# Other addresses for the low halves of the weights, and another order of products in layer two, in a two-layer hybrid encoder trunk

## The chip, the cores and the metric

The kernel runs on one core of one Trainium2 chip, as one launch. The metric is the device time of a launch in microseconds. Three timed runs stand for the kernel before, and one further execution was recorded by the profiler; all durations of single instructions come from that one.

## What is computed

The reference is a trunk of two layers on 256 tokens plus 16 learned meta tokens, with a model width of 2048. Cut to what matters:

```python
def _layer(h, ...):
    proj = einsum('bld,dp->blp', h, w_in)            # 2048 x 6176: GLA q, k, v, gate, decay and NA q, k, v
    y_gla = _gla_mixer(...)                          # bidirectional gated linear attention, 4 heads
    y_na = _na_mixer(...)                            # 2-D neighbourhood attention, 16 heads
    mix = einsum('blm,md->bld', concat([y_gla, y_na]), w_out)
    h = layer_norm(ALPHA * h + mix)
    ff = square(relu(h @ w_ff1)) @ w_ff2             # 2048 -> 8192 -> 2048
    return layer_norm(ALPHA * h + ff)
```

Everything is float32. By far the most arithmetic lies in the four weight matrices `w_in`, `w_out`, `w_ff1` and `w_ff2`; attention and norms are small beside them.

## The kernel before

**Split products.** A float32 product is made of products in a reduced format (float32r). Each weight tile and each activation tile is split into a high half (a rounding cast) and a low half (the rest). The sum is `wh*xh + wh*xl + wl*xh`. Activations lie transposed, 128 features on the partitions and tokens along the free axis, so a weight block of 128x128 is the stationary operand and 256 to 274 columns of tokens are the moving one.

**Weight tiles.** The stream of weights (`order`, line 153) is cut into tiles of 128 partitions x 1024 floats, that is eight blocks of 128x128. `made` (line 180) issues the DMA of a tile into `raw` on the SP queue, and `halves` (line 208) casts it to `wh` on ACT (line 211, L211 in the profile) and subtracts `raw - wh` into `wl` on DVE (line 212, L212). Each of `raw`, `wh` and `wl` has three buffers, and `weights` (line 174) keeps two tiles ahead of the one in use.

**Where a block lies.** `blocks` (line 194) gives the place of block j within the tile's row in SBUF: `first + j//2 * pair + j%2 * step` floats. For `wh` that is `0, 128, 256, ...`, blocks one behind the other. For `wl` the three numbers come from `LOWS` (line 42), by whether the tile is one of layer two's "once" tiles. Since `pair` is 320 floats (1280 bytes), the blocks of a tile stand at two places past a multiple of 256 bytes, by turns. Before the change these are 64 and 192 bytes for "once" tiles, and 0 and 192 bytes for all others. The start of each `wl` tile is a multiple of 256 bytes, and so are the starts of `wh` blocks.

**Two forms of the products of a tile.** `by_m` (line 276 on) makes one output tile after another, each from all its weight tiles. For each weight tile it calls `eight` (line 232), which runs through the string in `TURNS` (line 43) and issues one product for each letter (L246 in the profile): `h` is `wh` with the high half of the activations, `l` is `wh` with their low half, `w` is `wl` with their high half.

- In layer one, with 272 tokens (a few groups with 274), and in those products of layer two that still need the meta tokens (272 or 258 columns) or that are named as slim, the string is `hlhlwwhlhlww...`: 24 products, four on `wh` and two on `wl` by turns.
- In layer two most outputs need 256 tokens only. There a tile is "once": high and low half of the activations are laid side by side, and one `h` product of 512 columns makes `wh*xh` and `wh*xl` together; `w` is a product of 256 columns. A tile has eight `h` and eight `w`. Before the change the string is `hhhhhhhhwwwwwwww`: all eight 512-column products, then all eight of 256 columns.

In layer two's attention the halves of the activations that feed these 512-column products stand 288 floats apart (`pair`, line 303, without `dense`), in its output projection and its MLP they are contiguous.

`by_k` (line 257 on, L272) is another form, in which one pair of blocks serves four outputs. It reads the same kind of tiles and isn't touched, but for the place of the odd `wl` blocks.

**What sets the order around it.** Instructions are recorded engine by engine. Between the weight tiles `pump` (line 124) gives steps of attention and norms to the engines; where layer-two attention stands in this, a scheduler may put neighbouring small instructions of ACT, DVE, POOL and SP in another order when PE's order changes.

Of the kernel before, what the change touches and what calls it, by code (L numbers as in the profile page):

```python
# [14 lines left out]
P = 128  # L15
# [23 lines left out]
PAD = 40  # L39
PITCH = 288  # L40
WIDE = 1280
LOWS = {True: (16, P + 32, 2 * P + 64), False: (0, P + 48, 2 * P + 64)}
TURNS = {True: "hhhhhhhhwwwwwwww", False: "hlhlwwhlhlwwhlhlwwhlhlww"}


class Pair(tuple):
# [10 lines left out]
class Trunk:  # L57
# [122 lines left out]
    def made(self, ap, ends, once):  # L180
# [4 lines left out]
        wh, wl = self.wp.tile([P, WB], F32R, name="wh", tag="wh"), self.wp.tile([P, WIDE], F32R, name="wl", tag="wl")  # L185
        wh, wl = self.blocks(wh, 0, P, 2 * P), self.blocks(wl, *LOWS[once])
        for c in map(slice, (0,) + ends, ends):
# [44 lines left out]
    def eight(self, ps, wh, wl, x, n, first, last, once):  # L232
# [5 lines left out]
        seen = dict.fromkeys("hlw", 0)  # L238
        for i, kind in enumerate(TURNS[once]):
            j = seen[kind]  # L240
# [3 lines left out]
            if once:  # L244
                rhs, o = (v.once, ps) if kind == "h" else (v[0][:, :T], ps[:, T:])
            mm(o, lhsT=self.block(w, j), rhs=rhs, start=first and not i, stop=last and i == len(TURNS[once]) - 1)  # L246

# [958 lines left out]
```

## Time and profile before

| what | value |
|---|---|
| median of three runs | 2359.66 us (2359.44 to 2359.98) |
| the profiled execution's own time | 2360.16 us |
| its span in the trace | 2358.4 us |
| granted TensorE clock, mean | 0.999 |
| PE busy, weight loads busy | 2348.3 us, 2234.0 us |
| DVE busy, ACT busy | 1523.6 us, 1213.4 us |
| matrix products issued | 18180 |

The span is the time from the first to the last instruction; 1.8 us of the execution's own time lie around it. A product is busy from its start to its modelled end, and since products are pipelined the busy times of neighbours overlap. The rate at which PE really goes is therefore read from starts: in the timeline view each row has the start of a group of equal neighbouring instructions (us), the busy time, and how many there are, and the difference of two starts divided by the number of products between them is the time per product.

### The profile page before, as it was taken

To read this page: it belongs to the slowest core of one execution; us is meant where nothing else is said; L and a number is where in the kernel's file an instruction comes from. 1 tells how busy PE (TensorE), PEld (TensorE's weight loads), DVE (VectorE), ACT (ScalarE), POOL (GpSimd) and SP (SyncE) were. 2 spreads that over 40 slices of the span, in tenths; PEclk is the share of its full clock that TensorE was granted. 3 is DMA by queue.
4 is the path that set the end of the run, shared out by engine and by line. 5 is a ranking of instruction groups with operands and counts; after the bars stand their busy time and mean duration, and the time that the engine had idled before them with its cause. 6 is when DMAs were issued, how large, how long until landed. Compare 5 with 4: busy or idle time off the path is not lost.

```text
span 2358.4 us, 44599 instructions
## 1 busy us (share of the span) xinstructions
PE 2348.3 (100%) x18180; PEld 2234.0 (95%) x18180; DVE 1523.6 (65%) x2432; ACT 1213.4 (51%) x2100; POOL 131.4 (6%) x200
## 2 busy tenths in 40 slices
PE   9999999999999999999999999999999999999998
PEld 9999999999999999999999999999988888888888
DVE  5588777775544455546567787778866545666655
ACT  5666664564433344444457666655654333444443
POOL 0021110110000000000020111100100000000000
PEclk9999999999999999999999999999999999999999
DMA  8454445555555555555555555456566666666664
GB/s 260 153 160 153 151 141 171 170 178 179 176 174 177 177 174 178 178 175 176 177 184 160 174 167 154 156 159 199 182 194 191 193 189 194 189 192 211 202 192 146
DMA packets 118301, 419.02 MB, mean 178 GB/s; under 512 B 13512, under 2 KB 14024, under 8 KB 118096
## 3 DMA queue, kind: packets, MB, share of 16 engines
q1 hardware_dynamic: 117808, 415.65, 56.4%
q8 instruction: 142, 2.33, 0.4%
q10 hardware_dynamic: 288, 0.52, 0.1%
q14 instruction: 63, 0.52, 0.1%
HBM read 414.03 MB, written 2.10 MB: 176 GB/s over the span
## 4 chain that ended last, share of the span: by engine, by line
PE 97%; DVE 2%; issue 1%; ACT 1%; POOL 0%; DVEq 0%; ACTq 0%; POOLq 0%
PE mm L246 85%; PE mm L272 6%; PE bg L272 1%; PE bg L783 1%; PE mm L722 1%; PE bg L583 0%; DVE wl L212 0%; PE bg L429 0%; PE mm L748 0%; DVE acc L1011 0%; ACT wh L211 0%; PE mm L472 0%; PE bg L909 0%; PE bg L634 0%; PE bg L664 0%
## 5 line engine op out<-in xcount | busy, mean ns | idle before, releaser
L212 DVE TENSOR_TENSOR wl<-raw,wh 128x1024 fp32r<-128x1024 f32 (+1 forms) x770 | 942.6, 1225 | 649.1 <-ACT wh L211 644.6
L211 ACT CAST wh<-raw 128x1024 fp32r<-128x1024 f32 (+1 forms) x770 | 805.1, 1047 | 926.8 <-PE mm L246 579.5
L246 PE MATMUL mm<-x,wh 128*128 128x272 f32 (+3 forms) x5376 | 990.5, 311 | 0.0
L246 PEld LDWEIGHTS mm<-x,wh 128*128 128x128 f32 x5376 | 798.4, 188 | 38.6 <-PE mm L722 0.6
L246 PE MATMUL mm<-x,wl 128*128 128x272 f32 (+3 forms) x3264 | 590.1, 284 | 0.0
L246 PEld LDWEIGHTS mm<-x,wl 128*128 128x128 f32 x3264 | 485.4, 188 | 11.4
L246 PE MATMUL mm<-y,wh 128*128 128x272 f32 (+2 forms) x2128 | 411.4, 322 | 0.0
L246 PEld LDWEIGHTS mm<-y,wh 128*128 128x128 f32 x2128 | 325.4, 188 | 22.0
L246 PE MATMUL mm<-u,wh 128*128 128x272 f32 (+2 forms) x1552 | 299.1, 321 | 0.0
L246 PEld LDWEIGHTS mm<-u,wh 128*128 128x128 f32 x1552 | 237.1, 188 | 16.0
L246 PE MATMUL mm<-y,wl 128*128 128x272 f32 (+1 forms) x1408 | 240.5, 282 | 0.0
L246 PEld LDWEIGHTS mm<-y,wl 128*128 128x128 f32 x1408 | 204.3, 188 | 6.4
L246 PE MATMUL mm<-u,wl 128*128 128x272 f32 (+1 forms) x1024 | 175.2, 282 | 0.0
L246 PEld LDWEIGHTS mm<-u,wl 128*128 128x128 f32 x1024 | 148.8, 188 | 4.7
L272 PE MATMUL mm<-x,wh 128*128 128x272 f32 (+1 forms) x512 | 73.5, 289 | 0.0
L272 PEld LDWEIGHTS mm<-x,wh 128*128 128x128 f32 x512 | 67.9, 191 | 0.0
L999 POOL TENSOR_SCALAR acc<-acc,vec 128x272 f32<-128x272 f32 (+1 forms) x24 | 41.9, 1751 | 273.9 <-DVE acc L1011 154.2
L871 DVE TENSOR_TENSOR acc<-acc,mm 128x256 f32<-128x256 f32 (+1 forms) x71 | 30.1, 424 | 38.9 <-PE mm L246 38.9
L560 ACT COPY U<-S 128x272 f32<-128x272 f32 (+1 forms) x104 | 41.0, 429 | 19.3 <-DVE S L569 18.3
L569 DVE TENSOR_TENSOR S<-S,dec 128x272 f32<-128x272 f32 (+1 forms) x112 | 46.1, 441 | 3.7 <-ACT U L560 3.1
L294 ACT CAST u<-ft 128x272 fp32r<-128x272 f32 (+1 forms) x64 | 26.1, 408 | 41.7 <-DVE ft L827 41.7
L571 POOL TENSOR_TENSOR dec<-dec 128x272 f32<-128x272 f32 (+6 forms) x56 | 29.9, 534 | 245.9 <-DVE S L569 245.9
(265 smaller groups left out, 1634.4 us busy)
## 6 DMA issues: line engine op xcount, KB each, us to landing
raw<-in_wff SPq DMA_DIRECT2D x512, 512.0 KB, 3.6
raw<-in_win SPq DMA_DIRECT2D x190, 512.0 KB, 3.9
raw<-in_wout SPq DMA_DIRECT2D x64, 512.0 KB, 3.6
nb<-in_nab SPq DMA_DIRECT2D x16, 352.0 KB, 4.1
xraw<-in_xT SPq DMA_DIRECT2D x7, 272.0 KB, 5.5
out<-out SPq DMA_DIRECT2D x5, 256.0 KB, 3.2
brow<-in_norm SPq DMA_DIRECT2D x4, 256.0 KB, 4.9
gw<-in_wup SPq DMA_DIRECT2D x4, 196.0 KB
```

What stands on the lines that cost most here:

```text
L211: self.nc.scalar.copy(h, r)
L212: self.wl = self.nc.vector.tensor_tensor(lo, r, h.bitcast(F32), ALU.subtract).ins
L246: mm(o, lhsT=self.block(w, j), rhs=rhs, start=first and not i, stop=last and i == len(TURNS[once]) - 1)
L272: self.nc.tensor.matmul(ps[g + m][:, :n], lhsT=self.block(parts[p][0], 4 * j + m), rhs=acts[k + j][parts[p][1]][:, :n], start=k + j + p == ...
L294: self.nc.scalar.copy(hi, src)
L560: nc.scalar.copy(U[:, lv % 4, j, :w].rearrange("p (n t h) -> p n t h", t=2, h=hb), bass.AP(S.tensor, S.offset + 2 * j * L, [S.ap[0], [2 * ...
L569: tt(o, o, totals(lv, odd, w), ALU.mult)
L571: nc.gpsimd.tensor_tensor(d[1], d[1], d[0], ALU.mult)
L722: nc.tensor.matmul(ps[hh][:, t * NKEY:t * NKEY + NKEY], lhsT=q[hs, NM + t * P:NM + t * P + P], rhs=k[hs, t, :], start=True, stop=True)
L783: nc.tensor.matmul(po[t][hs, :P], lhsT=v2[ts, hs] if rest else v1[:, t, hs], rhs=p2[ts, hh, :] if rest else p1[:, 2 * hh + t, :], start=re ...
L871: tt(a, a, part, ALU.add)
L999: nc.gpsimd.tensor_scalar(a, a, gain, bias, ALU.mult, ALU.add)
```

## The change

Three numbers and one string differ. The low blocks of "once" tiles move from 64 and 192 bytes past a multiple of 256 to 32 and 160. The odd low blocks of all other tiles move from 192 to 64; the even ones stay at 0. And in "once" tiles the eight `h` and eight `w` products alternate: the two products of block 0, then those of block 1, and so on. The number of instructions of these kinds, their shapes and their operands stay the same, and so do the sums, apart from the order in which they are added.

```diff
-LOWS = {True: (16, P + 32, 2 * P + 64), False: (0, P + 48, 2 * P + 64)}
-TURNS = {True: "hhhhhhhhwwwwwwww", False: "hlhlwwhlhlwwhlhlwwhlhlww"}
+LOWS = {True: (8, P + 32, 2 * P + 64), False: (0, P + 16, 2 * P + 64)}
+TURNS = {True: "hwhwhwhwhwhwhwhw", False: "hlhlwwhlhlwwhlhlwwhlhlww"}
```

The code that reads the two tables is unchanged:

```python
wh, wl = self.blocks(wh, 0, P, 2 * P), self.blocks(wl, *LOWS[once])
...
for i, kind in enumerate(TURNS[once]):
```

## The prediction

> **What bounds the kernel now.** I read the page first: the busy times, the granted clock, and the chain that ended last.
>
> ```profile
> span 2358.4 us, 44599 instructions
> ...
> PE 2348.3 (100%) x18180; PEld 2234.0 (95%) x18180; DVE 1523.6 (65%) x2432; ACT 1213.4 (51%) x2100; POOL 131.4 (6%) x200
> ...
> PEclk9999999999999999999999999999999999999999
> ...
> PE 97%; DVE 2%; issue 1%; ACT 1%; POOL 0%; DVEq 0%; ACTq 0%; POOLq 0%
> ```
>
> PE is never without work, its clock is full in every slice, and 97% of the chain is PE. No other engine's work or wait is worth anything unless it stops PE. So the only question is how fast PE goes through products whose number and shape don't change. For that I read starts in the timeline, first in layer two's MLP (512- and 256-column products, ACT and DVE rows of the weight split between them).
>
> ```profile
> 1801.18 1.08 PE L246 MATMUL mm<-x,wl 128*128 128x256 f32 x8
> ...
> 1802.09 2.00 PE L246 MATMUL mm<-x,wh 128*128 128x512 f32 x8
> ...
> 1803.93 1.08 PE L246 MATMUL mm<-x,wl 128*128 128x256 f32 x8
> 1804.18 1.05 ACT L211 CAST wh<-raw 128x1024 fp32r<-128x1024 f32 x1 [1.40 <-issue]
> 1804.85 2.00 PE L246 MATMUL mm<-x,wh 128*128 128x512 f32 x8
> ...
> 1805.26 1.22 DVE L212 TENSOR_TENSOR wl<-raw,wh 128x1024 fp32r<-128x1024 f32 x1 [1.19 <-ACT wh L211]
> ...
> 1810.35 2.00 PE L246 MATMUL mm<-x,wh 128*128 128x512 f32 x8
> ```
>
> A tile's eight `h` take 1803.93 - 1802.09 = 1.84 us, 230 ns each; its eight `w` take 0.91 to 0.92 us, 114.3 ns each. From 1802.09 to 1810.35 are three tiles: **2.753 us a tile**. The same sixteen products in layer two's attention:
>
> ```profile
> 1458.19 2.02 PE L246 MATMUL mm<-x,wh 128*128 128x512 f32 x8
> 1460.04 1.11 PE L246 MATMUL mm<-x,wl 128*128 128x256 f32 x8
> 1460.99 2.02 PE L246 MATMUL mm<-x,wh 128*128 128x512 f32 x8
> 1462.84 1.11 PE L246 MATMUL mm<-x,wl 128*128 128x256 f32 x8
> ```
>
> Here a tile takes 1460.99 - 1458.19 = **2.80 us**: `w` 0.95 us (118.8 ns each), `h` 1.85 us. Same instructions, same weight addresses; what differs is that the halves of the activations lie apart. Next, the 272-column products: two stretches with the same string, one in layer two's attention (timeline), and layer one's long ones (the windows view: from:to, length, PE busy and count).
>
> ```profile
> 1448.45 0.41 PE L246 MATMUL mm<-x,wl 128*128 128x272 f32 x2
> 1448.69 0.65 PE L246 MATMUL mm<-x,wh 128*128 128x272 f32 x4
> ...
> 1454.31 0.41 PE L246 MATMUL mm<-x,wl 128*128 128x272 f32 x2
> ```
>
> ```profile
> 393.00:531.00 138.00, 138.00 (x1104) 138.00 (x1102) 106.42 (x183) 78.43 (x129) 14.59 (x8) 1.00 0.56 176
> 531.00:1071.00 540.00, 540.00 (x4329) 540.00 (x4328) 271.56 (x306) 222.44 (x299) 0.00 (x0) 1.00 0.56 177
> 1071.00:1222.00 151.00, 151.00 (x1209) 150.82 (x1209) 92.10 (x143) 66.31 (x88) 2.21 (x9) 1.00 0.59 184
> ```
>
> From 1448.45 to 1454.31 are eight sixes, 48 products: 122.1 ns each. In layer one 829 us hold 6642 products: 124.8 ns each. PE doesn't wait in either, the shapes are equal, and yet one rhythm is 2.2% slower. The lesson of these views is that a product costs its columns and then some nanoseconds that depend on how products and weight loads follow each other. This is the part of the time that the change can touch, and its size is the whole argument.
>
> **The change part by part.** How many tiles are there? Products of 512 columns (groups of the whole trace; the last row is the attention's part, 1222 to 1580 us):
>
> ```profile
> L246 PE MATMUL mm<-x,wh 128*128 128x512 f32 x1152 | 289.8, 394 | 0.0
> L246 PE MATMUL mm<-y,wh 128*128 128x512 f32 x688 | 172.5, 392 | 0.0
> L246 PE MATMUL mm<-u,wh 128*128 128x512 f32 x496 | 124.1, 392 | 0.0
> ...
> L246 PE MATMUL mm<-x,wh 128*128 128x512 f32 x320 | 81.6, 397 | 0.0
> ```
>
> 2336 / 8 = 292 tiles: 40 at 2.80 us and 252 at 2.753 us.
>
> *The turns.* Now every `w` follows an `h` and every `h` a `w`. The trace shows how an `h` run settles (cuts of the timeline begun within the run that starts at 1804.85):
>
> ```profile
> 1805.32 0.62 PE L246 MATMUL mm<-x,wh 128*128 128x512 f32 x2
> ```
>
> ```profile
> 1806.01 0.84 PE L246 MATMUL mm<-x,wh 128*128 128x512 f32 x3
> 1806.69 0.28 PE L246 MATMUL mm<-x,wl 128*128 128x256 f32 x1
> ```
>
> The third `h` starts at 1805.32, the sixth at 1806.01, the first `w` at 1806.69: the first two `h` take 0.47 us (235 ns each), the first five 1.16 us (232 ns), the last three 0.68 us (227 ns). An `h` just after a `w` is dearer than one in a settled run. For `w` in mixed order there is the slim group at the end, the string of threes with 256 columns in all products:
>
> ```profile
> 2334.36 0.40 PE L246 MATMUL mm<-y,wl 128*128 128x256 f32 x2
> 2334.59 0.64 PE L246 MATMUL mm<-y,wh 128*128 128x256 f32 x4
> ...
> 2345.00 0.40 PE L246 MATMUL mm<-u,wl 128*128 128x256 f32 x2
> ```
>
> 15 sixes in 10.64 us: 118.2 ns a product of 256 columns, against 114.3 ns in a run of eight `w`. So I price the alternating tile at 8 x (231 + 118.2) = 2.794 us: `w` by the mixed row, `h` between the run's mean of 230 and the 232 of its first five. That is +0.041 us on 252 tiles and -0.006 us on 40: **+10.1 us**.
>
> *The low blocks at 32 and 160.* No row shows a block at such a place, so I give it no term of its own, and bound the two edits together. Below: all `h` as the last three of a run, all `w` as in a run of the MLP, 8 x (227 + 114.3) = 2.730 us; that is -0.023 x 252 - 0.070 x 40 = -8.6 us. Above: all `h` as the first two (235), all `w` as in the attention (118.8): 2.830 us, +0.077 x 252 + 0.030 x 40 = +20.6 us. I take the price above since its rows are those in which products of two kinds alternate.
>
> *The odd low blocks from 192 to 64* in all other tiles touch one of six products in a 272-column tile. Bounds: all 6642 products of layer one in the quicker rhythm, 6642 x 2.7 ns = -18 us; above, I know no slower rhythm of a long stretch and set +9 us, half of that, as an estimate. The row nearest to it is layer one as it is, with low blocks at 0 and 192 and the quicker rhythm for some stretches already; the view shows no step that moves with one product in six. I take 0.
>
> *Splitting the weights.* ACT's cast for a later tile (1804.18) begins when the last `h` of a tile has ended; that `h` now stands 15th of 16 and not eighth, so the cast, and DVE's subtraction behind it, begin about 0.9 us later. Behind them in ACT's and DVE's queues wait casts and sums of outputs, and behind the freed `raw` SP's next weight DMA. The subtraction of 1805.26 ends at 1806.48; with three buffers its tile follows the one that starts at 1802.09 by three, so it starts at 1810.35, which leaves 3.9 us now and 3.0 us then, although the first `w` is needed one `h` after the tile's start and no longer eight. The cover is large, so this costs nothing; if it were gone, each tile would pay up to the 0.9 us. The next DMA for `raw` has the same three tiles. Reordered small instructions of attention lie under PE's work.
>
> Sum: 2360.16 + 10.1 = 2370.3 us in the terms of the profiled execution, whose time is 0.5 us over the median shown; so **2369.8 us** for the median.
>
> **A rule against it.** The Trainium skill, "TensorE: Matmul & The Clock Gate", section "Step-by-step: what each phase is for", says that moving operand and weight load have read ports of their own, so that loading weights takes nothing from the running product. By that rule neither address nor order would matter, and the time would stay at 2359.7 us. The trace doesn't bear it out fully: 122.1 against 124.8 ns per product at equal shapes. It is the third rival below, worked out from rows.
>
> **The rivals.**
>
> 1. *The alternation settles, and the loads agree with it.* An `h` run settles at 227 ns after five products at 235 to 230, so there is a timing of loads and products in which nothing is in the way, and a pattern of two products that repeats eight times could find it, the more so with low blocks moved by 32 bytes. For it: settling is seen. Against it: in the mixed rows (118.2 ns) and in the attention (118.8 ns) it never comes. Time: 2359.7 - 8.6 = 2351 us. It decides as soon as the tile falls under 2.753 us, that is when an alternating pair costs less than 344 ns.
> 2. *Layer one drops into its quicker rhythm*, since a sixth of its loads changes place. For it: both rhythms exist at equal shapes, and the slower one now holds 829 us. Against it: five of six loads stay. With the price of the turns: 2359.7 + 10.1 - 18 = 2352 us; without, 2342 us.
> 3. *Nothing changes.* The extra nanoseconds don't depend on order and place in the mean; 2359.7 us. For it: by the column, the runs (230 ns for 512, 114.3 for 256) and the quicker mixed stretch (122.1 for 272) cost nearly the same, 0.447 to 0.449 ns. Against it: the rows of the run's beginning and end.
>
> **How the numbers follow.** The forecast (slower, 2369.8 us; its own range 2360 to 2380) gets 0.46, the first rival 0.20, the second 0.18, the third 0.16. 0.2% is about what a measurement of this kernel can tell from no change, 4.7 us. The range: the forecast's upper bound is 2359.7 + 20.6 = 2380.3 us; below, it takes in rivals one and two with the layer-one gain alone at 2342 us, and a little for both together in part. Range 2340 to 2381 us. Faster 0.38, within 0.2% 0.16, slower 0.46.
>
> **What would show it.** In the changed profile, rows of one `h` and one `w` by turns in the MLP: sixteen products from 2.79 us apart would bear the price out, 2.73 the first rival, 2.753 the third. In layer one the same windows: 540 us for about 4330 products if it stays, about 4420 for the second rival. PE should still be busy throughout, and ACT's cast should begin just after a tile's last pair. The prediction is wrong if the alternating pair costs less than 344 ns, if layer one changes its rhythm, or if PE waits for `wl` at the start of tiles.

## The result, and the profile after

The changed kernel takes **2354.45 us** (median of 11 runs, 2353.12 to 2355.44) against 2359.44 us (median of 11 runs, 2358.78 to 2360.56): a ratio of 0.9978, with a 95% interval of 0.9968 to 0.9987. It is 5.0 us faster. A loss of 10 us was forecast; the time lies inside the stated range and next to the second rival's 2352 us.

The page of the profile after, the lines that answer to those of before:

```profile
span 2353.0 us, 44603 instructions
...
PE 2342.2 (100%) x18180; PEld 2222.5 (94%) x18180; DVE 1528.2 (65%) x2432; ACT 1213.0 (52%) x2100; POOL 130.2 (6%) x200
...
PE 96%; DVE 1%; ACT 1%; DMA 1%; issue 0%; SPq 0%; DVEq 0%; ACTq 0%
```

As many products as before, and PE idles as little as before (2353.0 - 2342.2 = 10.8 us, and 2358.4 - 2348.3 = 10.1 us before). So the pace has changed, and in two places in opposite ways. The windows view of layer one (from:to, length, PE busy and the number of products in brackets):

```profile
393.00:531.00 138.00, 138.00 (x1111) 138.00 (x1111) 106.79 (x182) 79.55 (x131) 14.58 (x8) 1.00 0.57 177
531.00:1071.00 540.00, 539.97 (x4418) 539.76 (x4417) 282.72 (x331) 230.12 (x313) 0.00 (x0) 1.00 0.57 179
1071.00:1222.00 151.00, 150.85 (x1227) 150.63 (x1226) 95.86 (x145) 70.79 (x98) 13.63 (x15) 1.00 0.58 185
```

In the long middle stretch 4418 products stand where 4329 stood: 122.2 ns a product, the quicker rhythm of before. Over the three windows 6756 products fit into the time of 6642. Later products have moved up into the windows, so what this is worth is better read from the starts of the same products in both traces: the 6635 that take 829.0 us before, from 393 us on, take 814.0 us after, 15.0 us less. Another 2.7 us come from layer one ahead of them. Layer two's MLP goes the other way (timeline after; ACT and DVE rows of the weight split between PE's):

```profile
1801.67 0.39 PE L246 MATMUL mm<-y,wh 128*128 128x512 f32 x1
...
1801.80 1.05 ACT L211 CAST wh<-raw 128x1024 fp32r<-128x1024 f32 x1 [1.45 <-issue]
...
1801.90 0.28 PE L246 MATMUL mm<-y,wl 128*128 128x256 f32 x1
...
1802.02 0.40 PE L246 MATMUL mm<-y,wh 128*128 128x512 f32 x1
...
1802.88 1.23 DVE L212 TENSOR_TENSOR wl<-raw,wh 128x1024 fp32r<-128x1024 f32 x1 [1.24 <-ACT wh L211]
...
1804.47 0.39 PE L246 MATMUL mm<-y,wh 128*128 128x512 f32 x1
```

A pair takes 0.35 us, an `h` 0.23 and a `w` 0.12, and the next tile begins at 1804.47: 2.80 us a tile, for 2.753 before. That is the tile that the prediction priced at 2.794.

### The profile page after: what moved, and what is told of

It reads as the page before. It is cut to its first block, busy times and chain, and to the rows that moved or that the text cites. A ratio compares the mean times of both kernels' runs of the same rounds, so it can differ in the third digit from the quotient of the medians.

```text
span 2353.0 us, 44603 instructions
## 1 busy us (share of the span) xinstructions
PE 2342.2 (100%) x18180; PEld 2222.5 (94%) x18180; DVE 1528.2 (65%) x2432; ACT 1213.0 (52%) x2100; POOL 130.2 (6%) x200
## 4 chain that ended last, share of the span: by engine, by line
PE 96%; DVE 1%; ACT 1%; DMA 1%; issue 0%; SPq 0%; DVEq 0%; ACTq 0%
PE mm L246 86%; PE mm L272 5%; PE bg L783 1%; DMA raw<-in_win 1%; PE mm L722 1%; PE bg L583 1%; DVE wl L212 0%; PE bg L272 0%; ACT wh L211 0%; PE bg L429 0%; DMA xraw<-in_xT 0%; PE mm L748 0%; DVE acc L1011 0%; PE bg L634 0%; PE bg L909 0%
## 5 line engine op out<-in xcount | busy, mean ns | idle before, releaser
L246 PE MATMUL mm<-x,wh 128*128 128x272 f32 (+3 forms) x5376 | 1099.3, 309 | 0.1
L246 PE MATMUL mm<-x,wl 128*128 128x272 f32 (+3 forms) x3264 | 753.4, 283 | 0.3 <-DVE wl L212 0.2
L246 PEld LDWEIGHTS mm<-x,wl 128*128 128x128 f32 x3264 | 548.3, 188 | 0.6 <-DVE wl L212 0.6
L246 PE MATMUL mm<-y,wh 128*128 128x272 f32 (+2 forms) x2128 | 477.3, 320 | 0.0
L246 PE MATMUL mm<-u,wh 128*128 128x272 f32 (+2 forms) x1552 | 347.0, 320 | 0.0
L246 PE MATMUL mm<-y,wl 128*128 128x272 f32 (+1 forms) x1408 | 338.8, 282 | 0.0
L246 PE MATMUL mm<-u,wl 128*128 128x272 f32 (+1 forms) x1024 | 246.1, 282 | 0.0
L246 PEld LDWEIGHTS mm<-y,wl 128*128 128x128 f32 x1408 | 242.2, 188 | 0.0
L246 PEld LDWEIGHTS mm<-u,wl 128*128 128x128 f32 x1024 | 176.2, 188 | 0.0
```

## The experiments

The diff changes two numbers and one string (not three numbers, as the section on the change says), and the experiments take them one by one. Each is the kernel before with the edit shown; from the turns alone on, each was timed once. The kernel before spread over 2358.4 to 2360.4 us in nine runs of the first set, so differences under about 1 us say nothing. To compare them I use the same two windows of each: 531 to 1071 us (layer one's MLP, 272 columns) and 1718 to 2218 us (layer two's MLP); 540 us divided by the first count is the time per product, 500 us times 16 divided by the second is the time per tile. Products that overlap an edge are counted, so both come out up to 0.1% low. For the second window of the kernel before and of the changed one:

```profile
1718.00:2218.00 500.00, 500.00 (x2908) 439.25 (x2907) 295.39 (x383) 222.17 (x288) 0.00 (x0) 1.00 0.63 196
```

```profile
1718.00:2218.00 500.00, 500.00 (x2859) 437.45 (x2858) 294.99 (x379) 219.97 (x288) 0.00 (x0) 1.00 0.61 192
```

### The odd low blocks alone

```diff
-LOWS = {True: (16, P + 32, 2 * P + 64), False: (0, P + 48, 2 * P + 64)}
+LOWS = {True: (16, P + 32, 2 * P + 64), False: (0, P + 16, 2 * P + 64)}
```

> Only the odd low blocks outside the 512-column tiles move, from 192 to 64; layer two's 512-column tiles stay as before. Theory (the place of the odd low block sets the rhythm of the 272-column products): layer one at 122.2 ns a product, layer two's MLP tile still 2.753 us, in all about 17 to 18 us under the kernel before, 2342 us. Rival (the two rhythms are a matter of the moment at which PE starts a stretch, and the place is of no account): layer one at 124.8 ns at least in part, 2350 to 2360 us.

Measured: 2341.55 us (median of 5 runs) against 2359.49 us, ratio 0.9926 (0.9912 to 0.9939). Its two windows:

```profile
531.00:1071.00 540.00, 539.98 (x4418) 539.76 (x4417) 282.76 (x333) 230.23 (x312) 0.00 (x0) 1.00 0.60 179
1718.00:2218.00 500.00, 500.00 (x2905) 438.96 (x2904) 300.39 (x397) 223.71 (x292) 0.00 (x0) 1.00 0.66 195
```

The first window equals that of the changed kernel (4418), the second that of the kernel before but for 3 products. So this one number gives -17.9 us, all the gain there is, and the rest of the change takes back 2354.45 - 2341.55 = 12.9 us. This version beats both kernels.

The gain isn't the cost of the one load that moved. From one start to the next, the six products of the string (`h l h l w w`) take 124.9, 125.6, 124.7, 126.2, 123.6 and 123.9 ns with the odd block at 192, and 124.2, 119.1, 120.9, 125.8, 120.9 and 122.5 ns at 64 (means from 540 to 1050 us of both traces). Only the last of the six uses the moved block, and most of the gain lies at the second and third.

### The turns alone, and the place at 32 and 160 alone

```diff
-TURNS = {True: "hhhhhhhhwwwwwwww", ...
+TURNS = {True: "hwhwhwhwhwhwhwhw", ...
```

> Only the order in the 512-column tiles changes to alternating; low blocks stand as before. Theory (the alternation itself costs): MLP tile 2.80 us, layer one still 124.8 ns, about 12 us over the kernel before, 2371 us. Rival (the place at 32 and 160 costs, the order is free or gains): tile 2.72 to 2.753 us, 2351 to 2360 us.

```diff
-LOWS = {True: (16, P + 32, 2 * P + 64), ...
+LOWS = {True: (8, P + 32, 2 * P + 64), ...
```

> Only the low blocks of the 512-column tiles move to 32 and 160, in the old order of runs. Theory (the alternation itself costs): tile 2.753 us, within 2 us of the kernel before. Rival (the place costs): tile 2.80 us, about 12 us over it.

Measured: 2377.78 us and 2372.26 us (one run each), 18.3 and 12.8 us over the kernel before. Windows of layer two of the turns alone, then of the place alone, and the place's timeline:

```profile
1718.00:2218.00 500.00, 500.00 (x2833) 433.50 (x2832) 292.09 (x375) 218.09 (x284) 0.00 (x0) 1.00 0.64 190
```

```profile
1718.00:2218.00 500.00, 500.00 (x2859) 438.14 (x2858) 290.87 (x376) 219.55 (x285) 0.00 (x0) 1.00 0.64 192
```

```profile
1802.45 2.01 PE L246 MATMUL mm<-x,wh 128*128 128x512 f32 x8
1804.30 1.11 PE L246 MATMUL mm<-x,wl 128*128 128x256 f32 x8
1805.25 2.01 PE L246 MATMUL mm<-x,wh 128*128 128x512 f32 x8
```

Here theory and rival are both half right, and the pair of experiments tells what neither said: each edit costs by itself, and they don't add. By tile: runs at 64 and 192 2.75 us, runs at 32 and 160 2.80, turns at 64 and 192 2.82, turns at 32 and 160 (the change) 2.80. In runs, the place costs the `w` (0.95 us for eight, 0.91 before) and hardly the `h` (1.85 for 1.84). Once the products alternate, 32 and 160 are the better place.

### Other places for the odd low blocks

```diff
-LOWS = {..., False: (0, P + 48, 2 * P + 64)}
+LOWS = {..., False: (0, P + 32, 2 * P + 64)}     # odd blocks at 128
+LOWS = {..., False: (0, P, 2 * P + 64)}          # in the next kernel: at 0
```

> Odd low blocks outside the 512-column tiles at 128, the rest as before. Theory (place sets the rhythm, each place its own): a rhythm of its own that holds through all of layer one, of which the theory says no number but that it differs from a mixture: anything from 120 to 127 ns. Rival (moment of the start alone): 122.2 and 124.8 ns both appear, by stretches, as in the kernel before.

> Odd low blocks outside the 512-column tiles at 0, like the even ones. If only the place within 128 bytes counted, this would go like 128: layer one at 125.5 ns a product, about 2369 us. If places count within 256 bytes: a rhythm of its own, not 125.5 ns.

Measured: 2369.29 us at 128 and 2361.35 us at 0. Layer one's window at 128, then at 0:

```profile
531.00:1071.00 540.00, 540.00 (x4303) 540.00 (x4302) 269.62 (x304) 222.93 (x300) 0.00 (x0) 1.00 0.59 175
```

```profile
531.00:1071.00 540.00, 540.00 (x4342) 540.00 (x4341) 272.12 (x308) 223.29 (x299) 0.00 (x0) 1.00 0.60 177
```

125.5 ns at 128 and 124.4 ns at 0: the rival that only the place within 128 bytes counts falls, and so it does by 64 (122.2) and 192 (124.7). Each place keeps one pace through the whole MLP of layer one. Of four places one sixth of the loads can have, the slowest and the quickest differ by 2.7%.

But this ranking is that of 272 columns. Between 455 and 485 us all four kernels run the same string with 274 columns; the windows with the odd blocks at 192 (before), 64, 128 and 0:

```profile
455.00:485.00 30.00, 30.00 (x241) 30.00 (x239) 28.89 (x48) 20.07 (x34) 12.68 (x7) 1.00 0.54 171
455.00:485.00 30.00, 30.00 (x239) 30.00 (x238) 27.97 (x47) 21.23 (x36) 14.57 (x8) 1.00 0.51 175
455.00:485.00 30.00, 30.00 (x237) 30.00 (x237) 28.90 (x47) 20.27 (x36) 12.44 (x7) 1.00 0.56 172
455.00:485.00 30.00, 30.00 (x235) 30.00 (x235) 28.28 (x48) 20.67 (x34) 12.67 (x7) 1.00 0.57 165
```

From starts this is 126.0, 126.7, 127.4 and 128.7 ns a product: here 192 is the quickest place and 0 the slowest. With 258 columns it is 121.1 ns at 192, 64 and 0, and 120.1 at 128.

### Is it the moment?

With the odd blocks at 192 the trace of before shows both rhythms. Two kernels have one more warm-up product at the start, so that PE's first real product begins later (4.78 us for 4.55):

```diff
-WARM = 14
+WARM = 15
```

> The kernel before with one more warm-up product at the start (15 for 14), so that all of PE's work begins some 0.1 to 0.2 us later; the extra product adds to nothing that is used. Theory (with odd blocks at 192 two rhythms can hold, and the moment at which a stretch begins picks one): the stretches of 122.2 and 124.8 ns fall otherwise than in the kernel before, total anywhere from 2343 to 2361 us. Rival (place alone decides, the quick stretches of before have another cause at their places in the program): the same stretches are quick, total within 1 us of the kernel before.

> Odd low blocks at 64 and one more warm-up product. Theory (at 64 only the quick rhythm holds, from whatever moment): 122.2 ns throughout layer one's MLP, 2341 to 2343 us. Rival (the moment picks the rhythm at 64 too): some stretches at another rate, 2344 us or more.

Measured: 2359.37 us (kernel before in the same set: 2359.36) and 2341.16 us. Layer one's window, first with blocks at 192, then at 64:

```profile
531.00:1071.00 540.00, 540.00 (x4329) 540.00 (x4328) 271.59 (x306) 222.05 (x297) 0.00 (x0) 1.00 0.59 177
```

```profile
531.00:1071.00 540.00, 539.98 (x4417) 539.76 (x4416) 282.93 (x333) 230.28 (x312) 0.00 (x0) 1.00 0.60 179
```

At 64 the quick rhythm holds as expected. At 192 the MLP's pace is unchanged, and this speaks for the rival. The delay itself doesn't last: the product that starts at 531.12 us before starts at 530.77 us here, earlier and not later. But other traces bear the rival out: from that product on the same 4326 products take 539.94 or 539.95 us in all four traces with 192 (before, this one, the turns alone, the place alone), and 528.73 us in all seven with 64, though in each group they begin at moments up to 1.8 us apart. Ahead of 393 us, where products of attention stand between the tiles, the draw does differ: one stretch that is slow in the kernel before is quick here, and also in the turns alone, whose layer one is the code of before. A last kernel disturbs PE in the middle of the stretch, by issuing one product as two of half the columns in the first tile of each group of four outputs (odd blocks at 192):

```diff
+            if i == 3 and self.kick and not once and n == L:
+                for c in (slice(0, n // 2), slice(n // 2, n)):
+                    mm(o[:, c], lhsT=self.block(w, j), rhs=rhs[:, c], start=False, stop=False)
+                continue
...
+                self.kick = m == 0 and not k and self.full
```

> The kernel before (odd low blocks at 192), but in layer one the fourth product of the first tile of each group of four outputs is issued as two of 136 columns, which computes the same and disturbs PE's rhythm for a moment. Theory (at 192 both rhythms hold once they are there, and a disturbance can put PE from one into the other): some of the stretches of layer one's MLP that run at 124.8 ns now run at 122.2 ns, up to 15 us under the kernel before. Rival (in the MLP only 124.8 ns holds at 192): 124.8 ns returns after each disturbance, 1 to 4 us over the kernel before.

Measured: 2358.84 us, 0.9 us under the kernel before in the same set (2359.71), one run each. The gain is too small to rest on, but the windows between neighbouring disturbances show what happens. First four of 22 us in a row, then four of 46 us:

```profile
521.00:543.00 22.00, 22.00 (x178) 22.00 (x177) 12.54 (x18) 10.46 (x17) 0.00 (x0) 1.00 0.58 169
544.00:566.00 22.00, 22.00 (x183) 22.00 (x182) 12.93 (x16) 9.92 (x16) 0.00 (x0) 1.00 0.61 183
568.00:590.00 22.00, 22.00 (x178) 22.00 (x178) 12.66 (x16) 9.60 (x14) 0.00 (x0) 1.00 0.64 184
591.00:613.00 22.00, 22.00 (x182) 22.00 (x181) 12.02 (x16) 10.55 (x16) 0.00 (x0) 1.00 0.59 176
...
639.00:685.00 46.00, 46.00 (x378) 46.00 (x378) 21.72 (x21) 16.75 (x18) 0.00 (x0) 1.00 0.59 182
687.00:733.00 46.00, 46.00 (x371) 46.00 (x370) 20.30 (x19) 15.76 (x15) 0.00 (x0) 1.00 0.57 177
735.00:781.00 46.00, 46.00 (x370) 46.00 (x370) 20.32 (x19) 15.76 (x15) 0.00 (x0) 1.00 0.61 176
783.00:829.00 46.00, 46.00 (x371) 46.00 (x370) 20.36 (x19) 15.75 (x15) 0.00 (x0) 1.00 0.59 177
```

178, 183, 178, 182 products: a disturbance throws PE from the slow rhythm into the quick one, and the next throws it back. Then 378, 371, 370, 371: three disturbances in a row end in the slow rhythm. From 543 us to the end of layer one, eight disturbances met the quick rhythm and all eight ended it; twelve met the slow one, and seven of them began the quick one. Which seven can be told from what PE did just before. The slow rhythm repeats every 18 products and the quick one every six, so a disturbance can fall at different points of the slow one. The last four distances ahead of the seven were about 122, 124, 123 and 124 ns, ahead of the other five 125, 127, 127 and 125 ns. So at 192 both rhythms hold until something disturbs them, and the point at which the disturbance falls picks one; at 64 no stretch of layer one's MLP runs in the slow one. Theory and rival of the pair above are thus joined: a local disturbance can draw the rhythm anew, and another moment for the start of the MLP didn't.

### Runs of two, and other places in layer two

All four kernels from here on have the odd blocks at 64, so the kernel to compare with is the first experiment (2341.55 us). It was timed in another set than these, but the kernel before took 2359.36 and 2359.71 us in their sets and 2359.49 in its own.

```diff
+TURNS = {True: "hhwwhhwwhhwwhhww", ...
```

> Odd low blocks at 64 as in the first experiment, and in the 512-column tiles (low blocks at 64 and 192) runs of two, hhww by turns, in place of runs of eight. Theory (the first products after a change of kind are the dear ones): a tile between 2.753 and 2.827 us, by the first two of each run in the kernel before 8 x (235 + 117) = 2.81 us, so about 14 us over the first experiment, 2356 us. Rival (alternation one by one is a case of its own): 2.753 us, 2342 us.

Measured: 2350.76 us. The tile is 2.78 us (2877 products in the window):

```profile
1718.00:2218.00 500.00, 500.00 (x2877) 436.90 (x2876) 297.96 (x386) 222.60 (x292) 0.00 (x0) 1.00 0.65 192
```

Between runs and turns, as the theory had it, but cheaper than its 2.81.

```diff
+LOWS = {True: (0, P + 16, 2 * P + 64), ...      # blocks at 0 and 64
+LOWS = {True: (0, P + 32, 2 * P + 64), ...      # at 0 and 128
+LOWS = {True: (24, P + 32, 2 * P + 64), ...     # at 96 and 224
```

> As the first experiment (odd blocks at 64 outside the 512-column tiles, runs of eight), but the low blocks of the 512-column tiles stand at 0 and 64. If the place sets the run's pace in these tiles too: a tile other than 2.753 us, between 2.72 and 2.83 us, total 2333 to 2361 us. Rival (64 and 192 are as good as any place on a 64-byte boundary, 32 and 160 only suffer from lying off it): 2.753 us, 2341 to 2343 us.

> As the one before it, with the low blocks of the 512-column tiles at 0 and 128, so that they keep the step of 640 bytes and are only shifted by 64. If the place counts: another tile time than 2.753 us. Rival (any 64-byte boundary is alike): 2.753 us, 2341 to 2343 us.

> As the one before it, at 96 and 224, off a 64-byte boundary like 32 and 160. If lying off the 64-byte boundary is what costs: 2.80 us a tile as at 32 and 160 in runs, 2353 to 2356 us. Rival (each place has its own pace): a tile other than 2.80 us.

Measured: 2348.88, 2351.27 and 2351.15 us. Windows of the first, the second, the third, and two pieces of the second's timeline:

```profile
1718.00:2218.00 500.00, 500.00 (x2880) 439.59 (x2879) 296.08 (x390) 222.59 (x291) 0.00 (x0) 1.00 0.65 193
```

```profile
1718.00:2218.00 500.00, 500.00 (x2869) 437.83 (x2868) 294.37 (x385) 221.93 (x290) 0.00 (x0) 1.00 0.65 192
```

```profile
1718.00:2218.00 500.00, 500.00 (x2869) 437.57 (x2868) 294.39 (x385) 222.12 (x290) 0.00 (x0) 1.00 0.64 192
```

```profile
1702.38 2.03 PE L246 MATMUL mm<-x,wh 128*128 128x512 f32 x8
...
1705.19 1.99 PE L246 MATMUL mm<-x,wh 128*128 128x512 f32 x8
```

```profile
2101.37 1.99 PE L246 MATMUL mm<-x,wh 128*128 128x512 f32 x8
...
2104.14 2.03 PE L246 MATMUL mm<-x,wh 128*128 128x512 f32 x8
```

2.78, 2.79 and 2.79 us in the mean; at 0 and 128 a tile of 2.81 us and one of 2.77 us stand in the same run, so more than one rhythm is there too. That blocks on a 64-byte boundary go well and others badly falls: both kernels with blocks on such boundaries are 7 to 10 us slower than the first experiment, and the one with 96 and 224, off such a boundary, goes like 0 and 128. 64 and 192 in runs of eight stay the best that was tried.

## Why the prediction was wrong

- **What bounds the kernel** was right: PE hardly pauses before (10.1 us) or after (10.8 us), and the difference is pace.
- **The step that failed** is "The odd low blocks from 192 to 64 ... I take 0", with its reason that the view shows "no step that moves with one product in six". It measured -17.9 us, close to the lower bound that the step itself had worked out from the two rhythms (-18). That the two agree so well is partly luck. The bound was meant for the 6642 products of the three windows, and there the trace of the first experiment gains 15.0 us; 2.6 us more come from layer one ahead of them and 0.7 us from layer two. Nor are the shapes in these windows equal, as the prediction says: 448 of the products have 274 columns and go slower at 64 (126.7 for 126.0 ns). The argument "five of six loads stay" was the mistake: the place of one load in six doesn't shift a cost of its own, it decides which rhythm the whole sequence can hold. The trace of before had shown that two exist and that the slow one filled layer one's MLP, which should have made that term, not the turns, the one to weigh.
- **The turns** were sized well: +10.1 us forecast, +12.9 us measured between the first experiment and the change; 2.794 us a tile forecast, 2.80 measured. Followed by the starts of the same products in both traces, 12.3 us of it lie behind layer one, where the two kernels differ, and most of that in the MLP's kind of tiles (252 x 0.047 = 11.8 us); 1.0 us lies ahead of 53 us, where they don't differ and where the traces with the odd blocks at 64 and the same warm-up differ among themselves by up to 1.4 us. But the step's picture was too simple. "The low blocks at 32 and 160" got no term, and alone they cost 12.8 us; the turns alone cost 18.3 us and not 10. The forecast hit their joint cost with rows of other products.
- **Splitting the weights** kept its cover in the MLP: the subtraction shown at 1802.88 us ends at 1804.11, and its tile starts at 1807.27, 3.2 us later, where 3.0 were forecast. The waits after, of PE's loads for DVE's subtraction in these products (us in total, times, longest):

```profile
PEld mm L246 <- DVE wl L212: 0.6, 2, 0.4
```

Both lie between 1222 and 1300 us, in layer two's attention; the kernel before and the first experiment have none, the turns alone have the same two. So the prediction's sign of PE waiting for `wl` did appear, but it is worth 0.6 us.

- **The first rival** (alternation settles) is refuted: the settled tile is 2.80 us. **The second** is what happened, with the price of the turns as it was stated: 2352 us by its working, 2354.45 measured. **The third** falls: in the first experiment shapes, order and counts are those of before and only the place of some loads differs, and the time falls to 0.9926 of it. The Trainium skill, "TensorE: Matmul & The Clock Gate", section "Step-by-step: what each phase is for", says that loading the next weights takes no SBUF read bandwidth from the running matmul. The prediction drew from it that neither address nor order would matter to the pace. That conclusion doesn't hold here; whether read bandwidth is the way in which the place acts, no run shows.

What stays open is how place and sequence make the rhythm. The runs show that it is so and how much it is, not by which step inside PE or the memory; the places of the `wh` blocks and of the activations were not tried. In the 272-column tiles the odd block's place and its distance from the even block move together (704, 576, 640 and 512 bytes for 192, 64, 128 and 0), and no run moves a block by a whole multiple of 256 bytes, so it isn't shown there that the place past a multiple of 256 is the right measure. In the 512-column tiles the place does count at a fixed distance of 640 bytes: 2.75, 2.80, 2.79 and 2.79 us a tile at 64, 32, 0 and 96.

## What to carry to other kernels

Where matrix products follow each other without a pause, read their pace from starts in the timeline, stretch by stretch; if equal shapes run at two paces, the slow one is a reserve, and the places of the stationary blocks are worth a sweep, for each number of columns by itself. Test each such edit alone: here one number was worth -17.9 us, and the two changed with it took 12.9 us back. And price neither place nor order by adding their single costs.

## What the runs showed of the hardware that was not expected

- Another place for the weight block of one product in six changes the pace of most of the six: 122.2, 124.4, 124.7 and 125.5 ns per 272-column product with the odd low blocks at 64, 0, 192 and 128 bytes past a multiple of 256. With 274 columns the same places give 126.7, 128.7, 126.0 and 127.4 ns, so the best place depends on the shape.
- The same sequence at the same places can hold two paces (122.2 and 124.8 ns). One split product can change from one to the other, for 22 to 46 us in the MLP, until the next: it ended the quick one in eight of eight cases and the slow one in seven of twelve.
- 512- and 256-column products in runs of eight at 64 and 192 take 2.75 us a tile, and 2.80 in the changed kernel, with PE busy through the whole window (500.00 of 500 us) at a granted clock of 1.00 in both.
